# adaLN sums of two d-tile blocks on TensorE instead of VectorE, and lookup tables traced earlier, in a two-layer hybrid mixer kernel

## The chip, the cores and the metric

The kernel runs on one core of a Trainium2 chip. The metric is the time of one execution on the device in microseconds; of several runs the median is taken. The core's engines each work through a list of their own and wait for one another by semaphores: TensorE (PE in the rows; its weight loads are PEld), VectorE (DVE), ScalarE (ACT), GpSimd (POOL) and SyncE (SP), whose queue issues most of the loads from HBM.

## The reference, cut to what matters

Two layers. Each takes a modulation from the condition `c` (adaLN), norms the tokens, scales and shifts them by the modulation, projects them by `w_in` (the kernel takes its columns in groups of 1024), runs three mixers on the parts and merges them.

```python
D_MODEL = 2048; SEQ = 256; DEPTH = 2
c_act = jax.nn.silu(c)
cos_ret, sin_ret = rope_tables(positions, RET_QK_DIM)
cos_mla, sin_mla = rope_tables(positions, MLA_ROPE_DIM)

def hybrid_layer(x, c_act, ada_w, ada_b, norm_pre, ...):
    mod = c_act @ ada_w + ada_b                       # ada_w: (2048, 3 * 2048)
    shift, scale, res_gate = jnp.split(mod, 3, axis=-1)
    h = rms_norm(x, norm_pre) * (1.0 + scale[:, None, :]) + shift[:, None, :]
    proj = h @ w_in
    ...                                               # three mixers, merge, output projection
    return x + (1.0 + res_gate[:, None, :]) * rms_norm(y, norm_post)
```

The RG-LRU mixer uses `softplus(-lambda)`, a vector of 1024 values for each layer.

## The kernel before

The 2048 channels of h are 16 d-tiles of 128. In layer 0 they come in five blocks, `KBLOCKS = [(0, 2), (2, 4), (4, 8), (8, 12), (12, 16)]`, called blocks 0 to 4 here. For each block the same six products run on TensorE (lx, lg, mqkv, mg and two of the merge logits, 1024 columns each), so that TensorE can begin when two d-tiles of h are there. In blocks 0 and 1 a product is one load of `w_in` of 1 MB (two d-tiles by 1024 columns), in blocks 2 to 4 it is two.

A load of `w_in` goes into one of four buffers `raw`. ScalarE casts it in two pieces to its 12-bit head `wh` (line 291), VectorE subtracts to get the exact rest `wl` (line 292), each into a ring of three. TensorE then multiplies head by head, head by rest and rest by head (lines 367 to 369 with columns on partitions, line 349 with tokens on partitions). VectorE adds a block's result to what the blocks before it gave (line 394); for block 0 ScalarE copies it (line 392).

The modulation of a block is made by `ada_block` from loads of `ada_w` into the same four buffers, 1 MB each: four loads in blocks 0 and 1 (8 rows of `ada_w` on each partition by 256 columns, twice for shift and twice for scale), eight in the others. Each row tile is multiplied by the value of `c_act` on its partition and added up: of each load VectorE takes all row tiles but two (lines 452 and 454), ScalarE multiplies the two others (line 445) and GpSimd adds them up (line 449). At the end VectorE joins both sums (line 458), TensorE transposes them (line 470), VectorE reduces over the partitions that are now columns (line 471), and `gains` makes the gain and shift vectors (lines 483 to 485). `h_tiles` transposes two d-tiles of the normed x (line 556), applies gain and shift (line 559), and ScalarE and VectorE split the result into head and rest (lines 567 and 568).

The order on TensorE and on SP's queue is the program order. The other three engines' order is set by a scheduler at build time. Side work is written as chains (generators), one step of which is traced after each load of a product: the chain `h1` makes block 1's modulation and h during block 0's products, and so on. `finish` traces a chain to its end. The chain `tables` makes the rope tables and the softplus vectors of both layers; it is started behind block 0's h, so its steps lie among block 0's products:

```python
start("h0", h_block(*KBLOCKS[0]))
for bi, kts in enumerate(KBLOCKS):
    finish(f"h{bi}")
    ...
    start(f"h{bi + 1}", h_block(*KBLOCKS[bi + 1]))
    if bi == 0:
        start("tables", tables())
```

Of the kernel before, what the change touches and what calls it, by code (L numbers as in the profile page):

```python
# [19 lines left out]
P = 128  # L20
D = 2048
T = 256
# [7 lines left out]
SHARE = {2: 2, 4: 2}  # L30
# [8 lines left out]
# per-layer vectors and their 128-blocks (ada_b: shift and scale only)  # L39
# [14 lines left out]
def hybrid_trunk(ctx: ExitStack, tc: tile.TileContext, a, out):  # L54
# [178 lines left out]
    def softplus_lambda(l):  # L233
        """8 * softplus(-lambda), and its negative"""
# [38 lines left out]
    def load_split(src, nk, ncol, spare=None):  # L273
        """heads and rests of a tile [128, nk, ncol], at most 1024 columns in a piece; in slots, listed in
        spare, if that is given"""
# [26 lines left out]
    class Act:  # L302
        """An operand [d, tokens], head and rest, in pieces of four d-tiles."""
# [21 lines left out]
    def gemm_x(act, w, r0, c0, kts, banks, ncol=W1, before=None, late=False):  # L325
        """tokens on partitions: banks[hf][j] += act.T @ w, the d-tiles in kts; yields after each tile.
        The first half of the tokens ends ahead of the second, by two tiles with late."""
# [25 lines left out]
    def gemm_w(act, w, r0, c0, kts, banks, before=None):  # L353
        """columns on partitions: banks[j][:, n, :] += w.T @ act for 8 blocks of 128 columns."""
# [21 lines left out]
    def act_slice(res, i):  # L376
        """The i-th 512 columns of a result held in two slots."""
        return res[i // 2][:, (i % 2) * 512:(i % 2 + 1) * 512]

    def group(act, w, c0, mode, kts, res, func, partial, before):  # L380
        """One product of 1024 columns into two slots (res, if given): token halves, or blocks 0-3 and 4-7."""
# [28 lines left out]
    def mean_of(ss):  # L410
        """sum of the parts / D + eps"""
        m = small([P, 1], "mean", 4)
        nc.vector.reduce_sum(out=m, in_=ss, axis=AX.X)
        nc.vector.tensor_scalar(m, m, 1.0 / D, EPS, ALU.mult, ALU.add)
        return m

    def square(src, acc, vector=False):
        """acc: the row sums of src ** 2, 512 columns"""
# [14 lines left out]
    def ada_sum(l, c0s, ncol, pause, share, use):  # L433
        """use(i, acc): acc is the sum over row tiles of c * ada_w for the ncol columns from c0s[i].
        Of the row tiles of a load, ScalarE and GpSimd take `share`, VectorE the others. Yields after each load."""
# [26 lines left out]
    def ada_block(l, k0, k1, pause, share):  # L462
        """gain and shift of the d-tiles k0..k1"""
# [11 lines left out]

    gvec, svec = [], []

    def gains(l, scale, shift, k0, k1):
        """norm gain and shift of the d-tiles k0..k1 from the adaLN sums."""
# [17 lines left out]
    def ada_res(l):  # L497
        """(1 + res_gate) * norm_post on every partition, in pieces of 512 columns"""
# [21 lines left out]
    def norm_of(xs):  # L520
        """1 / rms of the rows of xs ([hf][2] slots)"""
# [15 lines left out]
    def normed(xs, xn, r, c0, c1, both=False):  # L537
        """xn = xs * r in the columns c0..c1, of one slot"""
# [8 lines left out]
    def h_tiles(l, xs, act, k0, k1):  # L547
        """d-tiles k0..k1 (one or two) of h"""
        n = k1 - k0
        b = mbank()  # L550
        t = half_slot()
        for i in range(n):
            kt = k0 + i
            for hf in range(2):
                src = xs[hf][kt // 8][:, (kt % 8) * P:(kt % 8 + 1) * P]
                nc.tensor.transpose(b[:, i * T + hf * P:i * T + (hf + 1) * P], src, ident)
# [6 lines left out]

    def split_to(act, k, n, t):
        """t: the d-tiles k..k + n, in SBUF or PSUM."""
# [695 lines left out]
```

## Time and profile before

| what | us |
|---|---|
| median of 3 runs (2019.4 to 2023.18) | 2019.5 |
| span of the profiled execution | 2016.0 |
| TensorE busy in it | 1932.3 (96%) |
| VectorE busy | 1399.9 (69%) |
| ScalarE busy | 991.0 (49%) |
| GpSimd busy | 181.6 (9%) |
| median less span | 3.5 |

The profile is of one execution. Its span runs from the first to the last instruction on the engines. A share of busy time is a mean over stages with different limits, so the stages are looked at one by one. A matmul is recorded with its whole pipeline, so rows that follow one another overlap, and the distance from start to start is what one of them costs. The number behind a `<-` in brackets is idle time ahead of the instruction and what ended it.

### The profile page before, as it was taken

The numbers are of one execution on the slowest core, as the hardware profiler recorded it, in microseconds if no ns is written. First come the engines' busy times: TensorE is split into PE (matmuls) and PEld (weight loads), VectorE is DVE, ScalarE is ACT, GpSimd is POOL, SyncE is SP. The second block draws the span as 40 slices with busy tenths as digits, with TensorE's granted clock in tenths as the row PEclk, the third lists the DMA queues.
The fourth block names the chain that finished last, engine by engine and source line by source line (L and its number), as shares of the span: only waits on it lengthen the run. The fifth ranks groups of instructions, "written<-read, shape, count | busy, mean of one in ns | idle before, by whom it ended". The sixth has DMA issues, their size and how long they took to land.

```text
span 2016.0 us, 25350 instructions
## 1 busy us (share of the span) xinstructions
PE 1932.3 (96%) x9980; PEld 1624.1 (81%) x9980; DVE 1399.9 (69%) x1812; ACT 991.0 (49%) x1286; POOL 181.6 (9%) x137
## 2 busy tenths in 40 slices
PE   2979999999999999999989999999999999999998
PEld 2867888778988888777879989888898888788886
DVE  7899989787877687767567754446565447786555
ACT  5744538644554544433454774444455444444443
POOL 2242401100000010102010010000000001010100
PEclk9989999999999999999989999999999999999999
DMA  8787863787867777776655555555554557778563
GB/s 294 260 285 272 304 234 120 272 291 245 297 236 252 266 255 259 277 271 217 222 198 189 173 181 188 188 178 181 171 192 147 198 186 250 246 270 282 187 210 125
DMA packets 156936, 456.98 MB, mean 227 GB/s; under 512 B 12144, under 2 KB 20336, under 8 KB 156816
## 3 DMA queue, kind: packets, MB, share of 16 engines
q1 hardware_dynamic: 153248, 443.44, 64.8%
q0 software_dynamic: 3424, 11.65, 1.9%
q8 instruction: 78, 1.28, 0.3%
q14 instruction: 42, 0.34, 0.0%
q10 hardware_dynamic: 144, 0.26, 0.0%
HBM read 451.13 MB, written 4.19 MB: 226 GB/s over the span
## 4 chain that ended last, share of the span: by engine, by line
PE 79%; DVE 11%; DMA 6%; ACT 2%; issue 2%; POOL 0%; SPq 0%; DVEq 0%; ACTq 0%; POOLq 0%
PE acc L349 59%; DMA raw<-in_ada_w 5%; DVE float L454 4%; DVE wl L292 4%; PE acc L368 4%; PE acc L369 4%; PE acc L367 4%; DVE float L394 1%; PE mi L714 1%; PE mi L713 1%; PE mi L871 1%; ACT wh L291 0%; POOL float L891 0%; DMA raw<-in_w_in 0%; PE mi L801 0%
## 5 line engine op out<-in xcount | busy, mean ns | idle before, releaser
L349 PE MATMUL acc<-wh,float32r 128*128 128x512 f32 x4064 | 1159.4, 400 | 4.7 <-DVE float L394 4.4
L292 DVE TENSOR_TENSOR wl<-raw,wh 128x1024 fp32r<-128x1024 f32 (+1 forms) x640 | 794.0, 1244 | 451.9 <-ACT wh L291 445.4
L291 ACT CAST wh<-raw 128x1024 fp32r<-128x1024 f32 (+1 forms) x640 | 666.0, 1042 | 826.0 <-PE acc L349 656.2
L349 PEld LDWEIGHTS acc<-wh,float32r 128*128 128x128 f32 x4064 | 759.2, 189 | 186.3 <-DVE float L394 8.4
L349 PE MATMUL acc<-wl,float32r 128*128 128x512 f32 x2032 | 651.8, 397 | 13.8 <-DVE wl L292 13.8
L349 PEld LDWEIGHTS acc<-wl,float32r 128*128 128x128 f32 x2032 | 381.9, 189 | 110.6 <-DVE wl L292 20.6
L454 DVE SCALAR_TENSOR_TENSOR float<-raw,c_act,float 128x512 f32<-128x512 f32 (+1 forms) x326 | 255.7, 786 | 62.6 <-DMA raw<-in_ada_w 57.9
L367 PE MATMUL acc<-float32r,wh 128*128 128x256 f32 x768 | 218.7, 285 | 5.0 <-ACT float32r L567 5.0
L368 PE MATMUL acc<-float32r,wh 128*128 128x256 f32 x768 | 217.2, 283 | 0.8 <-DVE float32r L568 0.8
L369 PE MATMUL acc<-float32r,wl 128*128 128x256 f32 x768 | 217.1, 283 | 0.7 <-DVE wl L292 0.6
L367 PEld LDWEIGHTS acc<-float32r,wh 128*128 128x128 f32 x768 | 147.2, 192 | 6.3 <-ACT float32r L567 5.8
L368 PEld LDWEIGHTS acc<-float32r,wh 128*128 128x128 f32 x768 | 147.0, 191 | 1.8 <-DVE float32r L568 1.4
L369 PEld LDWEIGHTS acc<-float32r,wl 128*128 128x128 f32 x768 | 146.9, 191 | 1.1 <-DVE wl L292 1.1
L449 POOL TENSOR_TENSOR float<-float,float 128x512 f32<-128x512 f32 (+1 forms) x49 | 70.9, 1448 | 112.5 <-ACT float L445 107.5
L1050 POOL TENSOR_TENSOR float<-float,float 128x512 f32<-128x512 f32 x32 | 52.7, 1663 | 258.5 <-DVE float L1047 243.0
L394 DVE TENSOR_TENSOR float<-acc,float 128x512 f32<-128x512 f32 x96 | 62.5, 682 | 2.8 <-PE acc L349 1.4
L445 ACT ACTIVATE float<-raw,c_act 128x512 f32<-128x512 f32 (+1 forms) x64 | 40.1, 664 | 31.6 <-DMA raw<-in_ada_w 31.5
L793 POOL DMA_DIRECT2D float<-in_ret_gn x4 | 2.3, 570 | 570.0 <-PE mi L739 371.4
L470 PE MATMUL mi<-ident,float 128*128 128x128 f32 x64 | 10.4, 303 | 41.2 <-DVE float L458 41.2
L470 PEld LDWEIGHTS mi<-ident,float 128*128 128x128 f32 x64 | 8.1, 154 | 43.4 <-DVE float L458 42.5
L398 ACT ACTIVATE float<-acc 128x512 f32<-128x512 f32 x56 | 31.7, 598 | 13.0 <-PE acc L349 12.8
L1047 DVE TENSOR_TENSOR float<-acc,float 128x512 f32<-128x512 f32 x48 | 31.8, 683 | 2.4 <-PE acc L349 2.2
(231 smaller groups left out, 1286.2 us busy)
## 6 DMA issues: line engine op xcount, KB each, us to landing
raw<-in_w_in SPq DMA_DIRECT2D x224, 1024.0 KB, 5.1
raw<-in_ada_w SPq DMA_DIRECT2D x96, 1024.0 KB, 6.9
raw<-in_w_branch SPq DMA_DIRECT2D x48, 1024.0 KB, 6.2
raw<-in_w_out SPq DMA_DIRECT2D x32, 1024.0 KB, 5.5
raw<-in_mla_w_ukv SPq DMA_DIRECT2D x8, 1024.0 KB, 6.0
raw<-in_mla_w_uq SPq DMA_DIRECT2D x8, 768.0 KB, 4.5
float<-in_x SPq DMA_DIRECT2D x8, 512.0 KB, 7.5
float<-in_k_decay POOLq DMA_DIRECT2D x4, 512.0 KB, 4.5
```

What stands on the lines that cost most here:

```text
L291: nc.scalar.copy(wh, raw[:, c0:c0 + n])
L292: nc.vector.tensor_tensor(out=wl, in0=raw[:, c0:c0 + n], in1=wh.bitcast(F32), op=ALU.subtract)
L349: mm(b[:, 0:w_n], x, ws[:, j * w_n:(j + 1) * w_n], start=st, stop=sp)
L367: mm(dst, wh[:, cs], act.H(kt), start=first, stop=False, skip_group_check=True)
L368: mm(dst, wh[:, cs], act.L(kt), start=False, stop=False, skip_group_check=True)
L369: mm(dst, wl[:, cs], act.H(kt), start=False, stop=last, skip_group_check=True)
L394: nc.vector.tensor_tensor(out=dst, in0=b, in1=dst, op=ALU.add)
L445: nc.scalar.activation(out=t, in_=src, func=AF.Copy, scale=c)
L449: nc.gpsimd.tensor_tensor(out=acc[1], in0=acc[1], in1=t, op=ALU.add)
L454: nc.vector.scalar_tensor_tensor(acc[0], src, c, acc[0], ALU.mult, ALU.add)
L1047: nc.vector.tensor_tensor(out=gate[hf][:, cs], in0=banks[hf][j], in1=gate[hf][:, cs], op=ALU.mult)
L1050: nc.gpsimd.tensor_tensor(out=dst, in0=dst, in1=gate[hf][:, cs], op=ALU.add)
```

## The change

`ada_block_pe` replaces `ada_block` for the blocks of two d-tiles, that is blocks 0 and 1. It takes the same four loads, in the same order. Of each load it multiplies every piece of 128 by 128 as the stationary operand with the one column `c_act[:, r]`, and adds up in PSUM: 8 row tiles x 2 d-tiles = 16 products a load, 64 a block, all in plain float32. The sums come out with channels on partitions, so `gains` reads them from PSUM, without the join, the transposes and the reductions. Blocks 2 to 4 keep `ada_block` with a share of 2.

`h_turn` is the transposes of `h_tiles` as a function of its own. In block 0 it is called ahead of the last of the four loads. And the chain `tables` is traced to its end behind the first step of `h0`, ahead of block 0's products.

```diff
-SHARE = {2: 2, 4: 2}
+SHARE = 2
...
+    def ada_block_pe(l, k0, k1, between=None):
+        n = k1 - k0
+        ncol = n * P
+        nr = 2048 // ncol
+        b = mbank()
+        loads = [(which, r0) for which in range(2) for r0 in range(0, NKT, nr)]
+        for which, r0 in loads:
+            if (which, r0) == loads[-1] and between is not None:
+                between()
+            c0 = which * D + k0 * P
+            raw = load_raw(ada_rows[l][:, r0:r0 + nr, c0:c0 + ncol], nr, ncol)
+            for i in range(nr):
+                for j in range(n):
+                    col = which * n + j
+                    mm(b[:, col:col + 1], raw[:, i * ncol + j * P:i * ncol + (j + 1) * P], ada_scalar(r0 + i),
+                       start=(which == 0 and r0 + i == 0 and j == 0), stop=(r0 + i == NKT - 1 and col == 2 * n - 1), skip_group_check=True)
+            yield 1
+        gains(l, b[:, n:2 * n], b[:, 0:n], k0, k1)
...
-    def h_tiles(l, xs, act, k0, k1):
+    def h_tiles(l, xs, act, k0, k1, b=None):
         n = k1 - k0
-        b = mbank()
+        if b is None:
+            b = h_turn(xs, k0, k1)
         t = half_slot()
-        for i in range(n):
-            kt = k0 + i
-            for hf in range(2):
-                src = xs[hf][kt // 8][:, (kt % 8) * P:(kt % 8 + 1) * P]
-                nc.tensor.transpose(b[:, i * T + hf * P:i * T + (hf + 1) * P], src, ident)
...
+    def h_turn(xs, k0, k1):
+        b = mbank()
+        for i in range(k1 - k0):
+            kt = k0 + i
+            for hf in range(2):
+                src = xs[hf][kt // 8][:, (kt % 8) * P:(kt % 8 + 1) * P]
+                nc.tensor.transpose(b[:, i * T + hf * P:i * T + (hf + 1) * P], src, ident)
+        return b
...
-            yield from ada_block(0, k0, k1, 1, SHARE.get(k1 - k0, 1))
+            turned = []
+            if k1 - k0 == 2:
+                yield from ada_block_pe(0, k0, k1, (lambda: turned.append(h_turn(xs, k0, k1))) if k0 == 0 else None)
+            else:
+                yield from ada_block(0, k0, k1, 1, SHARE)
             k = k0
             while k < k1:
                 n = 1 if k % 2 else min(2, k1 - k)
-                h_tiles(0, xs, H, k, k + n)
+                h_tiles(0, xs, H, k, k + n, turned.pop() if turned else None)
...
             start("h0", h_block(*KBLOCKS[0]))
+            named["h0"].step()
+            for _ in tables():
+                pass
...
-                if bi == 0:
-                    start("tables", tables())
```

On TensorE, at the program's start, the kernel before has two transposes for each of shift and scale, four of x, and then block 0's first product (its line 367 begins with the head of h and the head of the first weight tile):

```order
L470 MATMUL mi_211<-ident,float_6_82 128x128 x2
L470 MATMUL mi_216<-ident,float_6_82 128x128 x2
L556 MATMUL mi_223<-ident,float_0_76 128x128
L556 MATMUL mi_223<-ident,float_2_78 128x128
L556 MATMUL mi_223<-ident,float_0_76 128x128
L556 MATMUL mi_223<-ident,float_2_78 128x128
L367 MATMUL acc_232<-float32r_98,wh_238 128x256
```

The same place in the changed kernel, where line 492 is the new one-column product, 16 to a load:

```order
L492 MATMUL mi_163<-c_act,raw_164 128x1 x16
L492 MATMUL mi_163<-c_act,raw_261 128x1 x16
L492 MATMUL mi_163<-c_act,raw_279 128x1 x16
L587 MATMUL mi_297<-ident,float_0_76 128x128
L587 MATMUL mi_297<-ident,float_2_78 128x128
L587 MATMUL mi_297<-ident,float_0_76 128x128
L587 MATMUL mi_297<-ident,float_2_78 128x128
L492 MATMUL mi_163<-c_act,raw_302 128x1 x16
L367 MATMUL acc_327<-float32r_98,wh_333 128x256
```

64 products stand where four transposes stood, and the transposes of x stand ahead of the last 16.

On TensorE, from block 0's first product to its second, the changed kernel (the kernel before goes from the first to the second without anything between):

```order
L367 MATMUL acc_330<-float32r_98,wh_337 128x256
L368 MATMUL acc_330<-float32r_99,wh_337 128x256
L369 MATMUL acc_330<-float32r_98,wl_338 128x256
L492 MATMUL mi_391<-c_act,raw_392 128x1 x16
L367 MATMUL acc_414<-float32r_98,wh_420 128x256
L368 MATMUL acc_414<-float32r_99,wh_420 128x256
L369 MATMUL acc_414<-float32r_98,wl_421 128x256
```

Block 1's sums stand here, 16 behind each of the first four products.

On ScalarE, ahead of block 0's first product, the kernel before casts the first weight tile (line 291) and then the head of h (line 567):

```order
L445 ACTIVATE float_12_88<-raw_198,c_act 128x256
L291 CAST wh_238<-raw_236 128x1024
L291 CAST wh_242<-raw_236 128x1024
L445 ACTIVATE float_15_91<-raw_297,c_act 128x256 x2
L567 CAST float32r_98<-float_13_89 128x512
```

The changed kernel, with the last rope tables, the norm of x and then the head of h (line 593):

```order
L221 ACTIVATE sinm<-float_6_82 128x2x32
L565 ACTIVATE float_0_76<-float_0_76,rstd_5_150 128x256
L565 ACTIVATE float_0_76<-float_0_76,rstd_5_150 128x512
L565 ACTIVATE float_1_77<-float_1_77,rstd_5_150 128x512 x2
L593 CAST float32r_98<-float_7_83 128x512
L291 CAST wh_333<-raw_331 128x1024
L291 CAST wh_337<-raw_331 128x1024
```

The casts of the first weight tile now stand behind the head of h.

## Rows read from the trace of the kernel before

**Rows 1.** Busy time of each engine by stretch, with granted clock, DMA share, GB/s:

```profile
0.00:38.60 38.60, 2.81 (x10) 1.73 (x10) 28.79 (x91) 20.47 (x37) 6.99 (x13) 1.00 0.92 302
38.60:77.40 38.80, 36.67 (x223) 32.98 (x224) 32.86 (x60) 28.74 (x51) 6.66 (x7) 1.00 0.77 263
77.40:130.70 53.30, 39.16 (x234) 33.02 (x232) 52.01 (x63) 26.36 (x34) 21.46 (x14) 0.91 0.81 281
130.70:2016.00 1885.30, 1853.70 (x9516) 1556.38 (x9516) 1286.28 (x1600) 915.43 (x1167) 146.46 (x103) 0.99 0.66 223
```

**Rows 2.** Timeline of ScalarE at the start: start, length, instruction, idle before:

```profile
14.56 1.28 ACT L241 ACT_TABLE_LOAD   x1
...
20.50 0.91 ACT L445 ACTIVATE float<-raw,c_act 128x256 f32<-128x256 f32 x2 [1.61 <-DMA raw<-in_ada_w]
23.42 0.91 ACT L445 ACTIVATE float<-raw,c_act 128x256 f32<-128x256 f32 x2 [2.02 <-DMA raw<-in_ada_w]
26.27 1.99 ACT L291 CAST wh<-raw 128x1024 fp32r<-128x1024 f32 x2 [1.94 <-DMA raw<-in_w_in]
```

**Rows 3.** Timeline of TensorE, block 0's first products:

```profile
38.97 0.41 PE L369 MATMUL acc<-float32r,wl 128*128 128x256 f32 x1
39.19 0.41 PE L367 MATMUL acc<-float32r,wh 128*128 128x256 f32 x1
...
42.38 0.32 PE L367 MATMUL acc<-float32r,wh 128*128 128x256 f32 x1
```

**Rows 4.** VectorE's largest group by shape, 0 to 77.4 us: count, busy us, mean ns:

```profile
L454 DVE SCALAR_TENSOR_TENSOR float<-raw,c_act,float 128x256 f32<-128x256 f32 x44 | 24.0, 550 | 0.3
```

**Rows 5.** Timeline of TensorE, the waits late in block 0:

```profile
60.92 0.38 PE L369 MATMUL acc<-float32r,wl 128*128 128x256 f32 x1 [0.60 <-DVE wl L292]
...
69.22 0.60 PE L470 MATMUL mi<-ident,float 128*128 128x128 f32 x4
71.34 0.66 PE L556 MATMUL mi<-ident,float 128*128 128x128 f32 x4 [1.52 <-DVE adac L471]
```

**Rows 6.** VectorE's groups by shape, 77.4 to 130.7 us:

```profile
L292 DVE TENSOR_TENSOR wl<-raw,wh 128x1024 fp32r<-128x1024 f32 x14 | 18.7, 1346 | 1.0 <-ACT wh L291 1.0
L454 DVE SCALAR_TENSOR_TENSOR float<-raw,c_act,float 128x512 f32<-128x512 f32 x14 | 15.5, 1126 | 0.1
L394 DVE TENSOR_TENSOR float<-acc,float 128x512 f32<-128x512 f32 x24 | 15.4, 678 | 0.0
```

**Rows 7.** Timeline of TensorE between blocks 1 and 2:

```profile
122.01 1.11 PE L470 MATMUL mi<-ident,float 128*128 128x128 f32 x4 [6.18 <-DVE float L458]
126.61 1.11 PE L470 MATMUL mi<-ident,float 128*128 128x128 f32 x4 [3.49 <-DVE float L458]
127.52 2.11 PE L556 MATMUL mi<-ident,float 128*128 128x128 f32 x8
```

**Rows 8.** Timeline of VectorE ahead of block 2:

```profile
127.06 0.75 DVE L454 SCALAR_TENSOR_TENSOR float<-raw,c_act,float 128x512 f32<-128x512 f32 x1
...
128.49 0.16 DVE L484 TENSOR_TENSOR gvec<-adac,vec 128x4 f32<-128x4 f32 x1
...
129.87 1.22 DVE L292 TENSOR_TENSOR wl<-raw,wh 128x1024 fp32r<-128x1024 f32 x1
```

**Rows 9.** Timeline of ScalarE ahead of block 2:

```profile
129.99 0.62 ACT L567 CAST float32r<-float 128x512 fp32r<-128x512 f32 x1 [1.28 <-DVE float L559]
```

**Rows 10.** Groups of matmuls and weight loads by shape, whole span: busy us, mean ns:

```profile
L814 PE MATMUL mi<-float,float 128*128 128x128 f32 x64 | 10.4, 275 | 0.0
...
L871 PEld LDWEIGHTS mi<-float,float 128*128 128x128 f32 x64 | 12.0, 190 | 1.8
...
L771 PEld LDWEIGHTS mi<-ident,float 128*128 128x128 f32 x64 | 7.8, 140 | 1.6
...
L948 PEld LDWEIGHTS acc<-float32r,wl 128*64 128x64 f32 x32 | 4.3, 135 | 0.5 <-DVE wl L292 0.5
```

**Rows 11.** Timeline of TensorE, eight float32 rows of 128 columns together:

```profile
734.23 1.05 PE L814 MATMUL mi<-float,float 128*128 128x128 f32 x8
```

## The prediction

> **What bounds the kernel now.** I read the stretches first [rows 1], cut at the three moments when a block of layer 0 starts on TensorE: 38.6 us (block 0), 77.4 us (block 1) and 130.7 us (block 2). From 130.7 us to the end TensorE is busy 1853.7 of 1885.3 us, so only what moves the start of block 2 can move the end. That the rest is untouched I take from the order of instructions: past layer 0's blocks every engine runs the same list in both kernels. The question is thus when block 2 starts.
>
> Before 38.6 us the chain of waits is VectorE's: it does the adaLN sums of block 0 row tile by row tile, and the last ada_w load is long on chip when TensorE starts: ScalarE stopped waiting for it at 23.42 us [rows 2], and the reader should see 15 us between that and the first product. From 38.6 to 77.4 us TensorE is the bound, 36.7 of 38.8 us busy [rows 1]; it waits 1.52 us for the sums of block 1 and 0.60 us once for a weight rest [rows 5]. From 77.4 to 130.7 us VectorE is the bound: 52.0 of 53.3 us busy [rows 1], with three groups (weight rests, adaLN sums of block 2, additions to partial results) making up 49.6 of it [rows 6]. TensorE stands idle at the end of that stretch, 6.18 and 3.49 us [rows 7].
>
> **The change, part by part.**
>
> *Sums of block 0 on TensorE.* VectorE, ScalarE and GpSimd lose their part of the sums of two blocks (on VectorE 44 multiply-add steps with 24.0 us of busy time up to 77.4 us [rows 4], and the joins and reductions behind them). TensorE gains 4 loads x 16 one-column products in each of the two blocks. A plain float32 product is two rows in the trace, each with a weight load of its own: L871 stands 32 times in the program and 64 times in the trace [rows 10]. So one block costs 4 x 16 x 2 = 128 pairs of weight load and matmul. What is the period of such a pair? No row shows a one-column product. Eight pairs with 128 columns take 1.05 us [rows 11], one of them 0.275 [rows 10], so (1.05 - 0.275) / 7 = 0.111 us from start to start. The weight load of 128 columns takes 0.190 us and one of 64 columns 0.135 [rows 10]: 64 columns make some 0.054, hence 128 make 0.107 us, and that share doesn't shrink with the moving operand. I take 0.107 us at full clock. At half clock the pairs of the main products stand 0.213 apart (38.97 and 39.19 us, 16 periods to 42.38 [rows 3]), and I take that there; that is the 1.2 GHz level, though the granted clock of that stretch reads 1.00, since TensorE works in little of it. The upper bound is a pair that overlaps nothing of its load: 0.190 us. The lower bound is 0.053, if the load ran like that of a transpose, whose 0.140 us is 0.05 less than 0.190 [rows 10].
>
> The fourth and last ada_w load of block 0 landed at 23.42 us, the third at 20.50 [rows 2], so the first at about 23.42 - 3 x 2.92 = 14.7 us. At half clock 128 pairs take 27.3 us, longer than the loads, so TensorE itself is the bound: 14.7 + 27.3 = 42.0 us, plus four transposes that now stand ahead of the last load's products, 0.9 us at half clock (1.11 for four with the tail [rows 7]), plus 0.2 us for the last one to drain (0.275 less a period): 43.1 us. Behind that: the three small VectorE instructions and the affine step, 1.5 us from 128.49 to 129.99 [rows 8, 9], and 0.2 for a third small one; 0.5 us until ScalarE is done with the head of h [rows 9]; and, since ScalarE now has the casts of the first weight tile *behind* that step, 1.0 us for one cast and 1.2 for its rest [rows 2, 8]. In the kernel before these two ran ahead, at 26.27 us [rows 2]. Sum 4.4 us, so 47.5 us against 38.97, the first product that reads a rest: **+8.5 us**.
>
> The loads, moved: an ada_w load's buffer is freed by TensorE and no longer by VectorE, so the first w_in load is issued after the first 32 pairs, at about 21.6 us instead of 20.30, and lands by some 27 us, long before 45. The rope and softplus tables move ahead of block 0: their small VectorE and ScalarE work, four more table loads (1.28 us each [rows 2]) and one small DMA on GpSimd's queue, moved ahead of GpSimd's additions, lie under the 27 us of one-column products and cost nothing; the table loads, 5.1 us, are the larger part, and without that cover up to this much would be added to the start.
>
> *Sums of block 1 on TensorE.* They stand between the products of block 0, 16 behind each of the first four, on the engine that is the bound. 128 x 0.107 = **+13.7 us** (6.8 to 24.3 by the bounds), nothing hides them. Behind each group of 16 the next main product waits, and the buffers that these free come later by as much. In return the four transposes with their reductions (69.22 to 71.34 [rows 5]) go, 2.1 us, and the 0.60 us stall on VectorE: **-2.7 us**.
>
> *Block 1.* Its work on VectorE is the same, and the loads of block 2's sums are issued as TensorE frees what is ahead of them, so this stretch moves with block 0. I give it VectorE's busy time, 52.0 instead of 53.3 us: **-1.3 us**.
>
> *Sum.* 8.5 + 13.7 - 2.7 - 1.3 = +18.2 us. The profiled execution has a span of 2016.0 us, 3.5 below the median of 2019.5; 2016.0 + 18.2 + 3.5 = **2037.7 us**.
>
> **What could go otherwise.**
>
> *W, the one-column stream raises the clock.* From their start at 38.6 us [rows 1] the main products ran at half clock until 42.38, 3.8 us [rows 3]. If the new stream does the same, 18 pairs run at 0.213 and 110 at 0.107: 14.7 + 3.8 + 11.8 = 30.3 us, 0.65 for transposes and drain, 4.4 behind: 35.4 us, a gain of 3.6 at the start. Sum -3.6 + 13.7 - 2.7 - 1.3 = +6.1: 2025.6 us. For it: TensorE is never idle in that stream. Against it: the nearest row, twelve transposes without a gap from 126.61 to 129.63, stayed at half clock, 2.11 us for the last eight [rows 7] where eight at full clock would take half.
> The Trainium skill's page "TensorE: Matmul & The Clock Gate" says under "What's actually happening" that "the default state is throttled, and activity releases the throttle", and under "Part 4: PE-mode transpose" that transposes don't count as busy in the same way as matmuls. By the first W would hold; by the second my nearest row says little of it. W keeps 0.29.
>
> *U, weight loads don't overlap.* 0.190 us a pair: 24.3 us in block 0, and a start at 14.7 + 24.3 + 0.65 + 4.4 = 44.1, 5.1 late; 5.1 + 24.3 - 4.0 = +25.4, 2044.9 us. Every float32 row so far overlaps, which speaks against it.
>
> *F, faster.* The pair's period is the transposes' 0.053 us. Then the loads are the bound at the start: 23.42 + 32 x 0.053 + 4.6 = 29.7, 9.3 early, and block 0 grows by 6.8: -9.3 + 6.8 - 4.0 = -6.5 us, 2013.0. In general the start is 23.42 + 32p + 4.6 and block 0 grows by 128p, together 160p - 14.9 us with the other two terms: it decides at p = 0.093 us. The loads that aren't transposes' take 0.190 us, which speaks against it.
> The page's table under "Back-to-back issue gap" gives products of 1 to 64 columns some 60 cycles, 25 ns; by that price the sum would be 160 x 0.025 - 14.9 = -10.9 us, an estimate. No float32 row here comes below 0.111.
>
> *G, block 1 catches up.* VectorE's 14 steps of sums there took 1.126 us each [rows 6] where an undisturbed one takes 0.75 [rows 8]; without these 5 us C falls to 2032.5 and W to 2020.5. Against it: GpSimd's additions beside them are unchanged.
>
> **How the numbers follow.** Half clock (C, 2037.7) 0.48; W 0.29; U 0.07; F 0.08; G 0.08 (0.05 on C, 0.03 on W). C has its own spread: a group of 16 is 3.4 us of one-column work, and TensorE lost its clock in 6.18 us without products (the transposes at 122.01 are already at half) but not in 1.52 [rows 5, 7]; should it lose it inside block 0, 3.8 us at half clock cost 1.9 each time, four times up to 7.6: 2045.3. A measurement here tells about 0.2%, 4.0 us, from no change. Faster takes F, 0.08. Same takes G on W and a W that comes out 2 us lower: 0.11. Slower 0.81. The range leaves out F and G on W below, and above what U or a lost clock would add beyond 2047: 2021 to 2047.
>
> **What would show it.** In the new trace: 32 rows of L492 to a load; their period in the first 30 us, 0.213 (C) or 0.107 (W); the first product that reads a weight rest at 47.5 (C) or 35.4 (W); block 1's first product at about 97 (C) or 85 (W), block 2's at about 149 (C) or 137 (W); groups of 3.4 us between the products of block 0; VectorE nearly idle before 40 us and just as full between blocks 1 and 2. I would be wrong if a product is one row, if the period is under 0.093 us, or if block 2's start doesn't follow block 1's by some 52 us.

## The result and the profile after

The changed kernel takes 2044.1 us (median of four runs, 2037.8 to 2047.8) against 2021.3 us for the kernel before (four runs, 2019.4 to 2023.9): the ratio is 1.0113, 95% interval 1.009 to 1.0135. The forecast was slower, 2037.7 us; the time lies inside the range and 6.4 us above the forecast. The profiled execution has a span of 2044.1 us, 28.1 above that of before (2016.0), where the medians differ by 22.8. Its own time is 2045.9 us, 1.8 more than its span and 1.8 above its median; by the same 1.8 the span of before belongs to an execution of some 2017.8 us (an estimate), shorter than all four of before. So the stretches below add up to 28 and not to 23.

First the busy time by stretch of the kernel after, cut at the first product that reads a weight rest and at the starts of blocks 1 and 2; the columns are those of [rows 1]: stretch, its length, busy time (and number of instructions) of TensorE, of its weight loads, of VectorE, ScalarE and GpSimd, then granted clock, DMA share and GB/s.

```profile
0.00:48.26 48.26, 28.98 (x134) 28.64 (x135) 16.46 (x75) 22.35 (x38) 2.14 (x7) 1.00 0.70 223
48.26:106.90 58.64, 58.64 (x346) 54.27 (x347) 18.11 (x21) 24.77 (x38) 1.46 (x1) 0.85 0.51 180
106.90:156.53 49.63, 38.35 (x233) 33.19 (x231) 48.81 (x63) 25.73 (x33) 22.23 (x14) 0.90 0.88 304
156.53:2044.10 1887.57, 1854.76 (x9516) 1556.02 (x9516) 1284.99 (x1600) 915.75 (x1167) 147.45 (x103) 0.99 0.65 223
```

Against [rows 1]: VectorE fell from 32.9 to 18.1 us in block 0, as the change intends, and TensorE is busy for all 58.64 us of it. The granted clock there is 0.85, where it was 1.00. Fifteen hundredths of 58.64 us are 8.8 us, and that is the larger part of what the forecast's sum doesn't have.

The start, from the timeline of TensorE (columns as in [rows 3]):

```profile
15.68 20.61 PE L492 MATMUL mi<-c_act,raw 128*128 128x1 f32 x96 [15.68 <-DMA raw<-in_ada_w]
36.15 1.09 PE L587 MATMUL mi<-ident,float 128*128 128x128 f32 x4
37.04 6.83 PE L492 MATMUL mi<-c_act,raw 128*128 128x1 f32 x32
47.00 0.58 PE L367 MATMUL acc<-float32r,wh 128*128 128x256 f32 x1 [3.14 <-ACT wh L291]
...
48.26 0.58 PE L369 MATMUL acc<-float32r,wl 128*128 128x256 f32 x1 [0.46 <-DVE wl L292]
```

32 rows to a load, 0.21 us apart from the first row to the last: the one-column stream ran 28 us at half clock. Then come the drain, the gains, h and the first weight tile, and the first product with a weight rest at 48.26 us.

The column of the granted clock doesn't show this: it reads 1.00 for the first stretch. The prediction put the 1.00 over [rows 3] down to TensorE working little there, but in the kernel before TensorE is busy for all 3.43 us from 38.97 to 42.40, at half clock, and the column reads 1.00 for these too. In these traces it shows half clock only after the first rise; until then the distance between the rows tells. So the 0.85 above leaves out the half clock at the beginning of block 0.

Inside block 0, the first group of block 1's sums (the 32 rows of one load) and what comes behind it:

```profile
56.37 3.63 PE L492 MATMUL mi<-c_act,raw 128*128 128x1 f32 x32
59.86 0.36 PE L367 MATMUL acc<-float32r,wh 128*128 128x256 f32 x1
...
60.65 0.28 PE L367 MATMUL acc<-float32r,wh 128*128 128x256 f32 x1
60.77 0.32 PE L368 MATMUL acc<-float32r,wh 128*128 128x256 f32 x1
60.88 0.42 PE L369 MATMUL acc<-float32r,wl 128*128 128x256 f32 x1
...
63.87 0.41 PE L368 MATMUL acc<-float32r,wh 128*128 128x256 f32 x1
64.08 0.37 PE L369 MATMUL acc<-float32r,wl 128*128 128x256 f32 x1
64.30 0.28 PE L367 MATMUL acc<-float32r,wh 128*128 128x256 f32 x1
...
81.30 0.52 PE L367 MATMUL acc<-float32r,wh 128*128 128x256 f32 x1
81.62 0.42 PE L368 MATMUL acc<-float32r,wh 128*128 128x256 f32 x1
...
89.84 2.81 PE L492 MATMUL mi<-c_act,raw 128*128 128x1 f32 x20
92.51 1.20 PE L349 MATMUL acc<-wh,float32r 128*128 128x512 f32 x2
```

The group itself runs at full clock, 32 rows in 3.49 us (56.37 to 59.86), 0.109 each. A microsecond behind it the main products go from 0.28 us each (0.117 apart) to 0.41 (0.213 apart), with no gap between them, and stay so until 64.1: TensorE never waited, and yet the clock fell. The clock falls at the other three groups too, but not always behind them: some 0.5 us behind the second (71.1 us), at the end of the third (81.3), and within the fourth, whose last 20 rows take 2.67 us where 2.18 would be full clock; there it stays down until 98.5.

### The profile page after: what moved, and what is told of

It is laid out like the page before. It is cut to its first block, busy times and chain, and to the rows that moved or that the text cites. A ratio compares the mean times of both kernels' runs of the same rounds, so it can differ in the third digit from the quotient of the medians.

```text
span 2044.1 us, 25747 instructions
## 1 busy us (share of the span) xinstructions
PE 1980.7 (97%) x10228; PEld 1672.1 (82%) x10228; DVE 1368.4 (67%) x1756; ACT 988.6 (48%) x1273; POOL 173.3 (8%) x125
## 4 chain that ended last, share of the span: by engine, by line
PE 78%; DVE 10%; DMA 8%; issue 2%; ACT 1%; POOL 0%; SPq 0%; DVEq 0%; POOLq 0%; ACTq 0%
PE acc L349 54%; DMA raw<-in_ada_w 8%; PE acc L369 4%; PE acc L368 4%; PE acc L367 4%; DVE float L454 4%; DVE wl L292 4%; PE mi L492 2%; DVE float L394 1%; PE mi L740 1%; PE mi L739 1%; PE mi L897 1%; PE mi L587 0%; ACT wh L291 0%; POOL float L917 0%
## 5 line engine op out<-in xcount | busy, mean ns | idle before, releaser
L292 DVE TENSOR_TENSOR wl<-raw,wh 128x1024 fp32r<-128x1024 f32 (+1 forms) x640 | 790.0, 1238 | 483.5 <-ACT wh L291 477.4
L291 ACT CAST wh<-raw 128x1024 fp32r<-128x1024 f32 (+1 forms) x640 | 666.0, 1042 | 822.8 <-PE acc L349 660.9
L349 PE MATMUL acc<-wl,float32r 128*128 128x512 f32 x2032 | 652.8, 398 | 13.7 <-DVE wl L292 13.5
L454 DVE SCALAR_TENSOR_TENSOR float<-raw,c_act,float 128x512 f32<-128x512 f32 x282 | 231.6, 824 | 70.3 <-DMA raw<-in_ada_w 65.9
L367 PE MATMUL acc<-float32r,wh 128*128 128x256 f32 x768 | 221.2, 288 | 4.8 <-ACT wh L291 3.1
L368 PE MATMUL acc<-float32r,wh 128*128 128x256 f32 x768 | 219.2, 285 | 0.5 <-DVE float32r L594 0.5
L367 PEld LDWEIGHTS acc<-float32r,wh 128*128 128x128 f32 x768 | 149.6, 195 | 5.7 <-ACT wh L291 3.2
L368 PEld LDWEIGHTS acc<-float32r,wh 128*128 128x128 f32 x768 | 149.5, 195 | 1.2 <-DVE float32r L594 0.8
L1081 POOL TENSOR_TENSOR float<-float,float 128x512 f32<-128x512 f32 x32 | 52.4, 1653 | 259.9 <-DVE float L1078 244.5
L449 POOL TENSOR_TENSOR float<-float,float 128x512 f32<-128x512 f32 x39 | 63.8, 1637 | 78.8 <-ACT float L445 77.6
L492 PE MATMUL mi<-c_act,raw 128*128 128x1 f32 x256 | 42.4, 301 | 15.7 <-DMA raw<-in_ada_w 15.7
L492 PEld LDWEIGHTS mi<-c_act,raw 128*128 128x128 f32 x256 | 42.6, 265 | 15.7 <-issue 15.6
L445 ACT ACTIVATE float<-raw,c_act 128x512 f32<-128x512 f32 x48 | 32.8, 719 | 20.9 <-DMA raw<-in_ada_w 20.9
```

The lines of the kernel that those rows point to most:

```text
L291: nc.scalar.copy(wh, raw[:, c0:c0 + n])
L292: nc.vector.tensor_tensor(out=wl, in0=raw[:, c0:c0 + n], in1=wh.bitcast(F32), op=ALU.subtract)
L349: mm(b[:, 0:w_n], x, ws[:, j * w_n:(j + 1) * w_n], start=st, stop=sp)
L367: mm(dst, wh[:, cs], act.H(kt), start=first, stop=False, skip_group_check=True)
L368: mm(dst, wh[:, cs], act.L(kt), start=False, stop=False, skip_group_check=True)
L445: nc.scalar.activation(out=t, in_=src, func=AF.Copy, scale=c)
```

## Experiments

Eleven kernels, in the order run. The edits are shown in part ("..." marks what is left out), against the changed kernel, for e3 and e11 against the kernel before, and for e8 and e9 against e7. Times are medians; a ratio is to the kernel before, with its 95% interval. The ratio of each was taken against the runs of before on its chip; the row of before has the median of all 27 of them, and after stands to the 2021.3 us given above. For every profiled execution the table gives the first product that reads a weight rest ("start"), the starts of blocks 1 and 2, and the span.

| kernel | start | block 1 | block 2 | span | median | ratio |
|---|---|---|---|---|---|---|
| before | 38.97 | 77.43 | 130.66 | 2016.0 | 2020.4 | 1 |
| after | 48.26 | 106.90 | 156.53 | 2044.1 | 2044.1 | 1.0113 (1.009 to 1.0135) |
| e1_block0_only | 47.84 | 88.02 | 140.15 | 2026.2 | 2028.8 | 1.0044 (1.0027 to 1.0062) |
| e2_block1_only | 38.91 | 97.26 | 150.36 | 2041.6 | 2042.0 | 1.0107 (1.0087 to 1.0126) |
| e3_tables_only | 44.57 | 81.18 | 133.65 | 2020.7 | 2022.7 | 1.0016 (1.0004 to 1.0028) |
| e4_spread | 48.09 | 98.83 | 150.08 | 2032.8 | 2034.5 | 1.0075 (1.0057 to 1.0093) |
| e5_wide_between | 56.17 | 114.53 | 168.02 | 2053.0 | 2053.5 | 1.0163 (1.0138 to 1.0189) |
| e6_casts_ahead | 46.78 | 104.45 | 158.12 | 2040.9 | 2044.3 | 1.012 (1.0099 to 1.014) |
| e7_block0_shared | 35.79 | 79.93 | 132.63 | 2018.2 | 2019.8 | 0.9995 (0.9982 to 1.0008) |
| e8_blocks0and2_shared | 36.67 | 79.97 | 128.14 | 2028.5 | 2027.0 | 1.0033 (1.0018 to 1.0047) |
| e9_shared_freq_early | 37.11 | 78.27 | 131.31 | 2019.7 | 2021.5 | 1.0006 (0.9997 to 1.0014) |
| e10_shared_wide | 37.71 | 77.50 | 130.18 | 2021.2 | 2023.0 | 1.0012 (1.0003 to 1.002) |
| e11_before_wide | 38.73 | 74.98 | 128.81 | 2014.8 | 2016.1 | 0.9976 (0.9965 to 0.9988) |

**e1, block 0 alone.**

```
-            if k1 - k0 == 2:
+            if k0 == 0:
                 yield from ada_block_pe(0, k0, k1, ...)
```

> Block 0's sums by one-column products on TensorE, block 1's sums on VectorE as in the kernel before, tables moved ahead. Theory A (the two blocks cost what the trace of after shows in each stretch: start +9.6 us, of block 0's +19.9 only the longer stretch at half clock at its beginning, about +1, and nothing given back): block 0's first product at 48 us, block 0 some 39 to 40 us long, total +10 to +11 us on the kernel before, 2031 to 2032. Rival B (a late start is given back, since loads and VectorE run ahead meanwhile and block 1 comes out shorter by what after shows, 3.7 us or more): 2025 to 2027. In both the clock stays up in block 0 once it has risen.

The stretch of block 0 in e1:

```profile
47.84:88.02 40.18, 37.53 (x222) 33.10 (x223) 32.85 (x48) 27.69 (x45) 7.17 (x7) 1.00 0.80 268
```

Start 8.9 us late, block 2 9.5 late, ratio 1.0044, some 9 us: one or two below the total of theory A, and above that of rival B. In the trace theory A holds: a late start isn't given back by block 2. No half clock inside block 0 after its beginning.

**e2, block 1 alone.**

```
-            if k1 - k0 == 2:
+            if k0 == 2:
...
-            named["h0"].step()
-            for _ in tables():
-                pass
+                if bi == 0:
+                    start("tables", tables())
```

> Block 1's sums by one-column products inside block 0, block 0's sums on VectorE and the tables as in the kernel before. Theory A: start at 38.6 us as before; four groups of 32 rows, 3.5 us each (14.0), less 2.7 us of transposes and stall, plus half clock behind each group, 8 us in all: block 0 some 58 us long, block 1 shorter by 2 to 4 us: +15 to +18 us, 2036 to 2039. Rival B (the clock is lost in after only because block 0 starts late and cold; from a start as before the groups leave it up): block 0 some 50 us, +8 to +11 us, 2029 to 2032.

From a start as before, block 1 begins 19.8 us late. The stretches of e2, columns as above, block 0 cut 0.4 us ahead of its first product with a weight rest (38.91):

```profile
0.00:38.53 38.53, 2.81 (x10) 1.72 (x10) 29.07 (x97) 19.58 (x34) 7.03 (x13) 1.00 0.94 301
38.53:97.26 58.73, 58.73 (x347) 54.35 (x348) 18.92 (x27) 27.48 (x45) 1.46 (x1) 0.85 0.49 165
```

The same clock of 0.85 and the same length as in after. Rival B falls: the groups take the clock down from the early start as well. The total (+21.6) is above the 15 to 18 expected; the part beyond block 2's start is 1891.2 us there against 1885.3, of which 3.2 us are longer waits of TensorE for weight rests (13.6 against 10.4) and 2.6 more busy time; why wasn't settled. It also means that the parts don't add: e1 and e2 delay block 2 by 29.2 us together, after delays it by 25.9.

**e3, the tables alone.**

```
             start("h0", h_block(*KBLOCKS[0]))
+            named["h0"].step()
+            for _ in tables():
+                pass
...
-                if bi == 0:
-                    start("tables", tables())
```

> The kernel before with the rope and softplus tables traced ahead of block 0, all sums on VectorE. Prediction's step (no cost under the one-column products, up to 5.1 us of table loads without that cover): here the cover is VectorE's sums, which run to about 36 us, and ScalarE has only 8 of its steps among them; between +0 and +5 us, 2021 to 2026, start of block 0 between 38.6 and 43.7. Rival: the tables' VectorE steps (some 8 us of small ones) stand ahead of the sums and push them all: start at 43 to 46 us, and what they leave free in block 0 is not needed there: +4 to +7 us, 2025 to 2028.

Start 5.6 us late, as the rival has it: VectorE begins its sums at 18.39 us behind the tables' small steps, at 15.31 in the kernel before. But block 0 then is 1.9 us shorter, since VectorE is rid of the tables there and TensorE waits 0.3 us for it instead of 2.1: block 1 3.8 and block 2 3.0 us late, the total by a ratio of 1.0016, some 3 us. So without the one-column products above them the tables cost 5.6 us at the start, more than the 5.1 us that the prediction allowed, and some 3 in the total; that this is ScalarE's table loads, as the prediction reasoned, isn't shown. Under the one-column products they cost nothing that shows.

**e4, the products spread.**

```
+                    later.append(product)
...
                     mm(dst, wl[:, cs], act.H(kt), start=False, stop=last, skip_group_check=True)
+                    emit(1)
```

> As after, but block 1's 64 products are spread through block 0 between the main products, one behind each three (L367 to L369) or two behind each six rows of L349, one tile later. Theory A (the clock falls because a group is 3.5 us of one-column work without a main product; spread thinly it stays up): no half clock inside block 0, some 8 us less: 2034 to 2038. Rival B (what counts is how much one-column work lies in a stretch, or each change between the two kinds costs time of its own): half clock remains or block 0 is as long as in after: 2042 to 2048.

The stretch of block 0 in e4, and its timeline of TensorE:

```profile
48.09:98.83 50.74, 50.74 (x346) 47.48 (x347) 18.28 (x21) 25.15 (x37) 1.46 (x1) 1.00 0.62 208
```
```profile
58.64 0.28 PE L499 MATMUL mi<-c_act,raw 128*128 128x1 f32 x2
58.78 0.36 PE L373 MATMUL acc<-float32r,wh 128*128 128x256 f32 x1
58.98 0.28 PE L374 MATMUL acc<-float32r,wh 128*128 128x256 f32 x1
59.11 0.28 PE L375 MATMUL acc<-float32r,wl 128*128 128x256 f32 x1
59.23 0.28 PE L499 MATMUL mi<-c_act,raw 128*128 128x1 f32 x2
```

The same 346 rows as in after, in another order: 50.74 us instead of 58.64, granted clock 1.00 instead of 0.85, and no row at half clock past the beginning. The clock lost at the groups thus cost 7.9 us; block 2 starts 6.5 us earlier, and the total falls by 9.6 us in the medians, 7.7 by the two ratios. Theory A holds: the grouping takes the clock down. Which property of the rows does it, their one column, their plain float32 or a weight load for each, no run separates; twelve transposes in plain float32 with 128 columns didn't raise the clock in 3 us either [rows 7].

**e5, wide products in the start's stream.**

```
+        for _ in range(24 if k0 == 0 else 0):
+            mm(idle, wide[:, 0:P], wide, start=True, stop=True)
...
+                if k0 == 0:
+                    mm(idle, wide[:, 0:P], wide, start=True, stop=True)
```

> As after, with wide products that compute nothing used: 24 bfloat16 products of 512 columns ahead of block 0's one-column stream (TensorE is idle there) and one behind each two one-column products in it, 32 in all. Theory A (the stream stays at half clock because it is one-column work; wide products raise the clock): 128 pairs at 0.11 and 32 wide ones at some 0.23 us are 21 us instead of 27.3, and the main products begin at full clock (3 us less): first product that reads a weight rest at about 42 us, block 0 as long as in after from there but for its cold start, total 8 to 9 us under after, 2035 to 2036. Rival B (the clock is held down in that stretch by something else, such as the time since the program began): 128 pairs at 0.213 and 32 wide ones at 0.43, 41 us: start at some 61 us, 2056 or more.

Neither came out. The timeline of TensorE in e5:

```profile
2.52 7.54 PE L488 MATMUL acc<-wide 128*128 128x512 bf16 x24 [2.52 <-POOL wide L477]
15.64 0.98 PE L498 MATMUL mi<-c_act,raw 128*128 128x1 f32 x4 [5.58 <-DMA raw<-in_ada_w]
16.48 0.59 PE L501 MATMUL acc<-wide 128*128 128x512 bf16 x1
16.86 0.85 PE L498 MATMUL mi<-c_act,raw 128*128 128x1 f32 x4
17.58 0.59 PE L501 MATMUL acc<-wide 128*128 128x512 bf16 x1
17.96 0.85 PE L498 MATMUL mi<-c_act,raw 128*128 128x1 f32 x4
```

24 wide products of zeros take 7.54 us: had all been at half clock (0.43 each, as ten such products take in e11, below) it would be 10. The first eleven of them take 4.74 us and the other thirteen 2.80, so the clock rose on the way, and nothing else holds it down this early (rival B's reason falls). After 5.58 us without work it is down, and one wide product behind each four rows doesn't bring it up in 35 us: one set follows the other every 1.09 us, to the end of the stream. So theory A is half right: wide products alone raise the clock, the one-column stream with one of them behind every four rows doesn't.

**e6, the first weight tile's casts ahead.**

```
+            if k0 == 0 and (which, r0) == loads[-1]:
+                early.append(load_split(wsrc(a["w_in"][l], 0, 0, 2, COL["lx"], W1), 2, W1))
...
+        with ExitStack() as order:
+            for ins in casts if k0 == 0 else ():
+                order.enter_context(tc.issue_after(ins))
+            gains(l, b[:, n:2 * n], b[:, 0:n], k0, k1)
```

> As after, but the first weight tile's two casts and two rests are put ahead of block 0's gains and of the head and rest of h on ScalarE and VectorE. By the prediction's step (in after these stand behind the head of h and cost 2.2 us of the start): first product that reads a weight rest at 46 us instead of 48.3, block 1's start earlier by the same, total 2 us under after: 2042. Rival (the start is given back later, since VectorE bounds block 1): no difference from after, 2044.

The start comes 1.5 us earlier (46.78), block 1 2.5 earlier, and block 2 1.6 us *later* than in after; the total is the same. Block 1 takes 53.7 us in e6 and 49.6 in after. Its groups on VectorE, in that stretch, of after and then of e6 (columns as in [rows 6]):

```profile
L292 DVE TENSOR_TENSOR wl<-raw,wh 128x1024 fp32r<-128x1024 f32 x14 | 18.0, 1298 | 0.7 <-ACT wh L291 0.7
```
```profile
L294 DVE TENSOR_TENSOR wl<-raw,wh 128x1024 fp32r<-128x1024 f32 x14 | 20.2, 1449 | 0.1
```

The same 14 weight rests, 1.30 us each in one and 1.45 in the other (2.1 of the 4.0 us), where those of the first 44 us take 1.22 in e7 and e11. The rival holds here: 2 us at the start are within what block 1's stretch moves by (49.6 to 53.8 us over all kernels with block 2's sums on VectorE). That GpSimd's additions beside them set this length fits, but wasn't tried apart.

**e7, block 0 shared out.**

```
+                    elif i < pe:
+                        for j in range(n):
+                            column(which * n + j, src[:, j * P:(j + 1) * P], c, False)
...
+            for i, t in enumerate(acc):
+                for j in range(n):
+                    column(which * n + j, t[:, j * P:(j + 1) * P], ones[:, 0:1], ...)
```

> Block 0's row tiles shared: of the 8 of each load TensorE takes 3 by one-column products, VectorE 3, ScalarE and GpSimd 2 as before; the partial sums of the latter are summed over partitions by one-column products with a column of ones (no transposes, no reductions). Block 1 and the tables as in the kernel before. Theory A (what made the start late was 128 pairs at half clock on one engine; shared out, the loads are the bound): last load at 23.4, 12 pairs and 8 more pairs at 0.213 behind it, 4.3 us, then 3 us to the first product: block 0 starts at 31 to 33 us, 6 to 7 us earlier, and as much off the total: 2013 to 2015. Rival B (the gain is given back, since the weight tiles of block 0 and the sums of block 1 come no earlier): block 0 longer by most of it, 2018 to 2021.

The start is 3.2 us earlier than before, not 6 to 7, and by block 1 (2.5 us later than before) it is more than given back: no difference in the total (0.9982 to 1.0008). Rival B. The largest piece of it, in block 0: VectorE's timeline, then TensorE's.

```profile
50.86 0.72 DVE L195 TENSOR_SCALAR float<-float,pos 128x96 f32<-128x96 f32 x1 [4.81 <-DMA float<-in_k_freq]
51.50 2.35 DVE L292 TENSOR_TENSOR wl<-raw,wh 128x1024 fp32r<-128x1024 f32 x2
```
```profile
52.77 0.74 PE L349 MATMUL acc<-wl,float32r 128*128 128x512 f32 x2 [2.86 <-DVE wl L292]
```

A rope step whose small load was late stood ahead of two weight rests on VectorE, and TensorE waited 2.86 us for these. Two more waits for weight rests, 0.84 and 1.69 us, follow in block 0, where the kernel before has one of 0.60.

**e8, block 2 shared out as well.** In the kernel of e7:

```
+            elif k0 == 4:
+                yield from ada_block_mix(0, k0, k1, 1, SHARE)
```

> As the kernel with block 0 shared, and in block 1's stretch, where VectorE is the bound, TensorE takes one row tile of the four of each load of block 2's sums (32 products, 64 pairs, in groups of 8 pairs) and sums the partial results over partitions by one-column products. Theory A (VectorE is the bound there: 8 of its 16 steps of 1.1 us and two reductions of 0.7 gone, 10 us; TensorE is given 7.5 us and has 14 us idle): block 1's stretch 45 to 47 us instead of 53, total 6 to 7 us under that kernel, 2006 to 2009. Rival B (the clock falls behind the groups, or GpSimd's additions become the bound): 2 us or nothing, 2011 to 2015.

Block 1's stretch falls to 48.2 us from 52.7, less than expected, and block 2 starts 2.5 us earlier than in the kernel before. But block 2's stretch grows from 76.2 us (130.66 to 206.83) to 86.4 (128.14 to 214.58), and the total is 7 us above e7. The gain was given back with interest one stage later. The trace says where: in block 2 TensorE stands idle for 9.7 us instead of 3.8, mostly for weight rests, which take 1.54 us each instead of 1.38, and its granted clock is 0.91 instead of 0.97. What slowed the rests stays open.

**e9, the rope frequencies loaded early.** In the kernel of e7:

```
+    freq = cpool.tile([P, NF], F32, name="freq")
+    nc.gpsimd.dma_start(out=freq, in_=a["k_freq"].partition_broadcast(P))
+
     def rope_tables():
...
-        nc.gpsimd.dma_start(out=freq, in_=a["k_freq"].partition_broadcast(P))
```

> The kernel with block 0 shared out, and the rope frequencies loaded at the program's start into a tile of their own. There the load stood behind GpSimd's additions, VectorE's first rope step waited 4.81 us for it, and the weight rests queued behind that step held TensorE up for 2.86 us. Theory A (that wait is where part of the earlier start went): the stall of 2.86 us is gone, block 1 starts at 77 us, the total falls by 2 to 3 us: 2017 to 2018. Rival (block 1's length makes it up again): no change, 2019 to 2021.

The stall is gone, block 1 starts 1.7 us earlier than in e7, the total isn't below it: the rival. Three shorter waits for weight tiles (1.26, 0.46 and 0.53 us) are what stands in block 0 now.

**e10 and e11, wide products where TensorE stands idle**, added to e9 and to the kernel before:

```
+    def keep(b, n):
+        for _ in range(n):
+            mm(b, wide[:, 0:P], wide, start=True, stop=True)
...
+            if (l, k0) == (0, 4):
+                keep(b, 12 if which else 24)
...
+                if bi == 0:
+                    keep(bank(), 10)
```

> As the kernel with block 0 shared out and the frequencies early, with wide bfloat16 products (512 columns, all ones, result not used) on TensorE where it would stand idle: 10 ahead of block 0's first main product, 24 and 12 ahead of the transposes for block 2's sums. Theory A (a run of wide products raises the clock or holds it, unlike one-column products with a wide one between): block 0 and block 2 begin at full clock, 2 to 3 us and 1 to 2 us less, total 3 to 5 us under that kernel, 2013 to 2015. Rival (they come too late or are too few, and delay what stands behind them): same or up to 3 us more.

> The kernel before with the same wide products in the same places and nothing else changed. Theory A (its 3.8 us and 2.5 us at half clock at the starts of blocks 0 and 2 are the price of a clock that fell while TensorE waited): 2 us less in block 0 and 1 to 2 us in block 2: 2017 to 2018, against 2020.9. Rival: no change, since block 1 is bound by VectorE and gives the first back: 2019 to 2021.

The timeline of TensorE in e11, at the start of block 0:

```profile
33.51 4.29 PE L483 MATMUL acc<-wide 128*128 128x512 bf16 x10
37.64 0.39 PE L367 MATMUL acc<-float32r,wh 128*128 128x256 f32 x1
38.50 0.39 PE L368 MATMUL acc<-float32r,wh 128*128 128x256 f32 x1 [0.48 <-DVE float32r L577]
38.73 0.28 PE L369 MATMUL acc<-float32r,wl 128*128 128x256 f32 x1
38.85 0.28 PE L367 MATMUL acc<-float32r,wh 128*128 128x256 f32 x1
```

Where [rows 3] has 0.41 us a product until 42.38, these run at 0.28 from 38.73 on. Block 1 begins 2.5 us and block 2 1.9 us earlier, and the median is 2016.1 us: below both kernels, by 0.24% (0.12 to 0.35) of the kernel before. Of the 4.3 us in the median the profiled execution shows these 1.9. At block 2 the clock was down again by its first products (0.41 us each), so the second half of theory A didn't come. In e10 block 0 also began at full clock, but it still waited 1.7 and 1.1 us for weight tiles, and the total isn't below e9: the rival.

## Why the prediction was right, and where its sum was short

*Who bounds what.* Right. Only the start of block 2 matters; all but 2.2 us of the 28.1 lie ahead of it (1887.6 us behind it in after, 1885.3 before).

*The sum.* +18.2 us was forecast for a span that grew by 28.1. The terms were off by +0.8 (start), +9.2 (block 0), -2.3 (block 1) and +2.2 us (behind block 2, put at nothing). By the spans the sum was thus 9.9 us short. That the median lies only 6.4 us above the forecast is in part luck: the forecast added 3.5 us from the span of before to its median, while the changed kernel's median equals its span, since the profiled execution of before was a short one and that of after a long one. Of the prediction's own places block 1 came at 106.90 us instead of about 97 and block 2 at 156.53 instead of about 149, 49.6 us behind it instead of some 52. The figure that came true is that of the side spread, 2045.3 us with the clock lost four times, and the range up to 2047 takes it in.

*The start, +8.5 us.* 9.3 measured. The pieces: the first load at 15.68 instead of 14.7; 128 pairs at half clock and four transposes 28.2 us (15.68 to 43.87) where 28.4 were forecast; 4.4 us behind them, as forecast. The case W (the stream raises the clock) didn't come, nor U (0.190 us a pair) or F (0.053): the period is 0.213 at half and 0.109 at full clock, forecast 0.213 and 0.107, and a product is two rows. The two weight loads that gave the 0.107 differ by 0.055 us, which doubled is 0.110. F took 0.053 for the transposes' period, but four of them take 0.60 us [rows 5], and less the 0.275 of the last one that is 0.108 from start to start. The nearest row decided rightly here, the twelve transposes that stayed at half clock [rows 7]. The rule of W, the Trainium skill's "TensorE: Matmul & The Clock Gate", "What's actually happening", that activity releases the throttle, doesn't hold for this activity: 96 rows without a gap in 20.6 us released nothing, while ten wide products in e11 did.
The price of 25 ns for products of 1 to 64 columns (the Trainium skill's "TensorE: Matmul & The Clock Gate", "Back-to-back issue gap") is under a quarter of the 0.109 us that one row together with its weight load takes here. The same page of the Trainium skill gives a weight load of P columns P / 1.2 ns ("LDWEIGHTS (loading the stationary operand)"), for 128 columns an estimate of 107 ns, which agrees with the rows at full clock, but not with the 0.213 at half.

*Block 0, +11.0 us.* This is the step that was mis-sized: 58.64 us against 38.46, +20.2. The 128 pairs cost 14.4 (three groups of 3.49 us and one of 3.93) instead of 13.7, and the transposes and the stall went as said. Missing in the sum is the clock. The prediction names it and gives it up to 7.6 us, "should it lose it inside block 0", but as a side spread, and puts it at nothing in the sum: it set 3.4 us of one-column work between the 1.52 us without products in which the clock stayed and the 6.18 us in which it fell [rows 5, 7], and gave neither outcome a chance. e4 measures the term: 7.9 us, with the same rows in another order. The remaining 1.3 us show in e4 too (50.74 against 38.46, +12.3); about 1 of it is the half clock at the beginning, 5.3 us long (48.64 to 53.97) instead of 3.4 [rows 3].
An order of evidence would have helped: the reading that one-column work doesn't raise the clock was given 0.48, and the same reading suggests that a group of it lets the clock fall, as an idle stretch does. The forecast used it at the start and not in block 0.

*Block 1, -1.3 us.* -3.6 in the profiled execution (49.6 us); the other kernels with the same work on VectorE there (all but e8) give 51.3 to 53.8, so the forecast is as good as this stretch can be told. G's saving of 5 us (block 1 catches up) didn't come as it was reasoned: the steps of L454 went from 1126 ns [rows 6] to 1010, not to 750.

```profile
L454 DVE SCALAR_TENSOR_TENSOR float<-raw,c_act,float 128x512 f32<-128x512 f32 x14 | 13.7, 1010 | 0.0
```

*The tables, nothing.* Right under the cover of the one-column stream; e3 shows what they cost without it, 5.6 us at the start and some 3 in the total, against up to 5.1 allowed.

*The casts behind the head of h, 2.2 us.* The place is right (3.14 us of wait for L291, 0.46 for L292) and e6 takes 1.5 us of it away at the start, but the total doesn't follow.

Open: why the part behind block 2 differs by some us between kernels that are alike there (1882.7 in e4, 1891.2 in e2; TensorE waits 3.6 us longer for weight rests in e2 and is busy 3.9 us longer), what slowed the weight rests of block 2 in e8, and which property of the one-column rows lets the clock fall.

## What to carry to other kernels

Before moving small sums to TensorE, price them by weight loads, not by columns, and ask what they do to the clock: a block of one-column products ran at half clock at the start, and inside a full stretch it took the clock down for the wide products behind it, which no wait in the profile shows. The granted clock of the stretch shows it, but not ahead of the first rise; the distance from row to row shows both. If such products must stand on the bounding engine, spread them thinly between the wide ones (7.9 us here for the same instructions). And an earlier start of one stage is worth only what the next bound lets through: four kernels here (e7 to e10) began 1 to 3 us earlier than the kernel before and ended no earlier.

## What the runs showed of the hardware

- A float32 product with one moving column is two pairs of weight load and matmul, 0.109 us a pair at full clock and 0.213 at half.
- TensorE's clock fell from full to half while it was busy without a gap: 3.49 us of one-column products, then main products at 0.117 us for about one more microsecond, then 0.213; at the fourth such group it fell before the group's end. With two such rows behind every three main products (0.235 us beside 0.351) it stayed up from 56 to 91 us (e4); with one wide product behind four such rows it never rose in 35 us (e5).
- Wide products of zeros (e5) and of ones (e11), with results that nobody reads, raise the clock: the kernel before with ten of them in idle time ahead of block 0, where it then began at full clock, and 36 ahead of block 2, where it still began at half, took 0.24% less.
- The profile's granted clock reads 1.00 ahead of the first rise, though the rows stand at half clock (0.213 us a pair from 15.68 us on in after); behind it, it follows the rows (0.50 from 15.6 to 52.0 us in e5).
